# Branch C's head norm in three background pieces, with its factors and the output gate's rows sent round by DRAM

## The chip, the core and the metric

One core of a Trainium2 chip runs the whole program. The metric is device time in microseconds (us) from launch to end, as the median of several runs. The engines are named as the profile names them: PE (TensorE, with PEld for its weight loads), DVE (VectorE), ACT (ScalarE), POOL (GpSimd) and SP (SyncE, which issues every DMA of this kernel). All arithmetic is fp32. Matrix products split each operand into a high and a low part and take three products (`mm3`).

## What is computed

A two-layer mixer over 1152 tokens (128 context tokens, then 1024 latent ones) and 1024 channels. Each layer has three branches A (windowed attention), B (a gated recurrence) and C (differential attention). What the change touches is the norm at the end of branch C, and the gate of the residual:

```python
def diff_attn(q, k, v, lam, subln, lam_init):
    ...
        s = jnp.einsum('bqhmd,bshmd->bhmqs', qblk, k).astype(jnp.float32) * SCALE
        p = jax.nn.softmax(s, axis=-1)
        pd = p[:, :, 0] - lam * p[:, :, 1]
        return jnp.einsum('bhqs,bshe->bqhe', pd.astype(v.dtype), v)
    ...
    o = rmsnorm(o, subln) * (1 - lam_init)        # per token and head, over 128 channels

def mixer_tail(x, gate, oa, g_a, ob, g_b, oc, g_c, merge, P):
    m = jax.nn.sigmoid(merge).reshape(B, T, N_BRANCH, D_MODEL)
    y = (m[:, :, 0] * ((oa * jax.nn.silu(g_a)) @ P['w_br_a'])
         + m[:, :, 1] * ((ob * jax.nn.silu(g_b)) @ P['w_br_b'])
         + m[:, :, 2] * ((oc * jax.nn.silu(g_c)) @ P['w_br_c']))
    return x + gate * (y @ P['w_out'])            # gate: one row of 1024, from the modulation
```

## The kernel before

Tokens are nine tiles of 128, channels and heads lie on the 128 partitions where a product needs them. A layer has four stages.

1. **The unit phase** (`unit_phase`). Four heads of C, then branch A's four groups. A foreground does the attention of head h over five groups of token tiles (`GR`): scores and their eviction (`c_probs`), then, one group late, transposes and the product with V (`c_pv`, run by `flush`). A background generator makes the next head's q, k and v (`qkv_gemm`: nine token tiles, every third followed by `qk_rows`), then the head's SiLU gate in three pieces (`gate_silu`). `step(n)` takes n pieces of the background between groups; `fg` runs the foreground under a priority raised by 2000 instructions.
2. **The tail steps** (`tail_step`): 22 steps of merge gates and branch projections, with branch B's recurrence (`lru`) beside them.
3. **`tail_last`**: the last two column blocks, which use both `T` buffers (`mg2`).
4. **`w_out_phase`**: four column quarters `q4`, each over nine token tiles i: 24 products of 256 columns into PSUM, then on DVE `tm = p * gr` and `x = x + tm`, then a store. In layer 0 the next layer's modulation (`mod_chunk`, long sums on DVE) and its normed input (`to_h`) are made in the same stage.

The instruction order is not the program's: a planner simulates the program and takes, on each engine, the ready instruction of highest priority (program order, less the raised offset); that order is then fixed, and each engine runs its own list in order. SBUF buffers come from rings (`RINGS`: S 26, P 7, T 2, W 7, D 3, E 2, cx 1), PSUM from three (`PSB`: s 4, t 3, o 1). A tile waits until a slot of its ring is free.

At the end of head h of C, `c_finish` (L580) runs in the foreground, when the group after its last product is flushed, in head h+1's second group. It squares O (L582, ACT, one piece of 1152), sums over partitions with nine products against a column of ones (L585), takes the inverse root on DVE (`rsqrt`, 14 small instructions), spreads the nine factors over partitions with nine products of a broadcast column against the identity (L593), scales O from that PSUM (DVE) and multiplies by the gate on POOL. In the trace each fp32 product of these two lines stands as two matmuls, so 18 and 18 for a head. O sits in the P ring, the gate in the S ring, until then.

`gate_rows` (L1035) makes the row tile `gr` (128 x 2 x 256) of a quarter in the same way: four products of a broadcast column against the identity (L1040), two ACT copies. `gr` lies in the single `cx` buffer, so a quarter's copies wait for the last tile of the quarter before. The `xt` tiles of `w_out_phase` rotate over the rings E, D, T (`XT`), and in layer 0's last quarter over E, T (`XT3`).

Of the kernel before, what the change touches and what calls it, by code (L numbers as in the profile page):

```python
# [10 lines left out]
F32 = mybir.dt.float32  # L11
# [7 lines left out]
DEPTH = 2  # L19
# [45 lines left out]
def hybrid_dit_kernel(ctx, tc, I, O):  # L65
# [14 lines left out]
    def al(tag, name, *shape):  # L80

        return big.tile([128] + list(shape), F32, tag=tag, name=name, bufs=RINGS[tag])
# [33 lines left out]


    xres = drp.tile([NT, 128, DM], F32, name="xres")
    osp = [drp.tile([4, 128, NTOK], F32, name=f"osp{b}") for b in range(3)]
    xsp, gsp = (drp.tile([4, 128, NTOK], F32, name=n) for n in ("xsp", "gsp"))  # L120

# [456 lines left out]
        acopy(u.o[:, tiles[0] * 128:tiles[0] * 128 + w], po)  # L578

    def c_finish(L, u, h):  # L580
        sq = al("T", "sq", 1152)
        A.activation(out=sq, in_=u.o, func=AF.Square)  # L582
        p = ps("t", 9)
        for i in range(9):
            T.matmul(out=p[:, i:i + 1], lhsT=sq[:, i * 128:(i + 1) * 128], rhs=one, start=True, stop=True)  # L585
        e2 = tl("e2", 9)
        stt(e2, u.l0, EPS, u.l0, ALU.mult, ALU.mult)
        y = rsqrt(p, 9, 1.0 / 128, e2)
        for c in range(3):
            pb = ps("t", 3, 128)  # L590
            for t in range(3):
                i = 3 * c + t
                T.matmul(out=pb[:, t, :], lhsT=y[:, i:i + 1].to_broadcast([128, 128]), rhs=ident, start=True, stop=True)  # L593
            oc = u.o[:, c * 384:(c + 1) * 384].rearrange("p (t n) -> p t n", t=3)
            stt(oc, oc, L.D.sub1, pb, ALU.mult, ALU.mult)
            tt(Pq, u.o[:, c * 384:(c + 1) * 384], u.o[:, c * 384:(c + 1) * 384],
               u.gate[:, c * 384:(c + 1) * 384], ALU.mult)
        dma(osp[2][h], u.o)

# [126 lines left out]
    def unit_phase(L):  # L728

        l = L.l  # L730
        a_groups = [CQA, CKA, CVA]
        pend = None

        done = None

        def flush():
            nonlocal pend, done
            d, done = done, None
            if pend:
                pend()  # L740
                pend = None
            if d:
                d()

        def start(h):
            u = Unit()
            if h < 4:
                L.units.append(u)
                return qkv_gemm(L, u, L.wu, (0, 1), O["nck"][0, l, :, h, :, :], O["ncv"][0, l, :, h, :],
                                V if h == 0 else None)  # L750
            L.ua = u
            return qkv_gemm(L, u, L.wu, (2, 3), O["nak"][0, l], O["nav"][0, l].rearrange("t v d -> t (v d)"))

        def background():

            for h in range(4):
                L.wu = load_wu(L, c_groups(h + 1) if h < 3 else a_groups)
                yield from start(h + 1)
                yield from gate_silu(L, CGC + 128 * h, lambda gate, u=L.units[h]: setattr(u, "gate", gate))
            L.wu2 = load_wu(L, [CQA + 128, CQA + 256, CQA + 384])  # L760
            yield from a_gemm2(L)
            for g in range(4):
                yield from gate_silu(L, CGA + 128 * g, L.gates.append)
                if g:
                    yield from lru_x(L, g - 1)
            yield from lru_x(L, 3)

        def step(n):
            for _ in range(n):
                next(bg, None)  # L770

        def fg(f, *args):
            with tc.high_priority(offset=HPO):
                return f(*args)
        for _ in start(0):
            pass
        bg = background()
        step(BG0[0])
        fg(c_kconv, L, L.units[0], 0)
        for h in range(4):  # L780
            u = L.units[h]
            u.l0 = tl("l0", 9, bufs=2)
            qn = BGQ if h else BG0
            if h:
                step(qn[0])
            fg(v_conv, u, I["cache_c_v"][0, l, :, h, :])
            for g, tiles in enumerate(GR):
                n = len(tiles)
                q = fg(q_conv, u.q[:, tiles[0]:tiles[0] + n, :, :].rearrange("p t m d -> p (t m) d"), 2 * n)
                Ps = [fg(c_probs, L, u, tiles[0], q, 0)]  # L790
                fg(flush)
                if n == 2:
                    Ps.append(fg(c_probs, L, u, tiles[1], q, 1))

                def pend(u=u, tiles=tiles, Ps=Ps, h=h, g=g):
                    if g == 0:
                        u.o = al("P", "O", 1152)
                    c_pv(L, u, tiles, Ps)
                    if g == 4:
                        nonlocal done  # L800
                        done = lambda: c_finish(L, u, h)
                step(qn[g + 1])
            if h < 3:
                fg(c_kconv, L, L.units[h + 1], h + 1)
            else:
                fg(a_kconv, L)
        u = L.ua
        fg(v_conv, u, I["cache_a_v"][0, l].rearrange("t v d -> t (v d)"), True)
        fg(flush)
        L.mask = al("P", "mask", 9, 128)  # L810
        dma(L.mask, I["mask"].rearrange("p (a b) -> p a b", a=9))
        step(BGA[0])
        for g in range(4):
            for n, tiles in enumerate(GR):
                i, m = tiles[0], len(tiles)
                q = fg(q_conv, (u.qs[g] if g else u.q)[:, i:i + m, :, :].rearrange("p t h d -> p (t h) d"), 2 * m)
                Ps = fg(a_probs, L, g, tiles, q)
                fg(flush)

                def pend(g=g, n=n, tiles=tiles, Ps=Ps):  # L820
                    if n == 0:
                        L.Oa = al("P", "Oa", 1152)
                    a_pv(L, g, tiles, Ps, L.Oa)
                    if n == 4:
                        nonlocal done
                        done = lambda o=L.Oa: a_finish(L, g, o)
                step(BGA[n + 1])
        fg(flush)
        fg(flush)
        for _ in bg:  # L830
            pass
# [200 lines left out]
                tail_branch(L, 2, j, c, ohl, wbs[j], ms[j - 6][:, c, :])  # L1032
                y_split(L, j, c)

    def gate_rows(D, q4, dst):  # L1035

        for s in range(2):
            p = ps("t", 2, 128)
            for k in range(2):
                T.matmul(out=p[:, k, :], lhsT=D.modt[:, 16 + 2 * q4 + k, s:s + 1].to_broadcast([128, 128]),  # L1040
                         rhs=ident, start=True, stop=True)
            acopy(dst[:, s, :], p.rearrange("p k n -> p (k n)"), scale=0.5)

    def x_in(l, i):
        if l:
# [14 lines left out]
    def w_out_phase(L, Ln):  # L1060
        l = L.l
        wtag = ("P", "S", "S", "P")
        wq = [load_wo(L, 0, wtag[0])]
        gr = None
        for q4 in range(4):
            cs = slice(q4 * 256, (q4 + 1) * 256)
            if q4 < 3:
                wq.append(load_wo(L, q4 + 1, wtag[q4 + 1]))
            w = wq[q4]
            gr = al("cx", "gr", 2, 256)  # L1070
            gate_rows(L.D, q4, gr)
            if q4 == 1 and Ln is not None:
                load_unit_consts(Ln)
                Ln.wu = load_wu(Ln, c_groups(0))
# [112 lines left out]
    for l in range(DEPTH):  # L1187
        L = Ls[l]
        L.mods = [(L.D, 16, 3), (L.D, 19, 3), (L.D, 22, 2)] if l == 0 else []
        layer_scalars(L.D)  # L1190
        if l + 1 < DEPTH:
            for _ in layer_vectors(l + 1):
                pass
            Dn = Ls[l + 1].D
            L.mods += [(Dn, b, 3) for b in range(0, 24, 3)]
        unit_phase(L)
        steps = [(2, 0, j) for j in range(8)] + [(0, 1, j) for j in range(8)] + [(1, 2, j) for j in range(6)]
        o = {}
        for n, (br, order, j) in enumerate(steps):
            if n == 0:  # L1200
                with tc.high_priority(offset=TPO):
                    o[2] = load_o(L, 2)
            if n in LRUN:
                with tc.high_priority(offset=LPO):
                    lru(L, LRUN.index(n))
            if n == 7:
                with tc.high_priority(offset=TPO):
                    o[0] = load_o(L, 0)
            if n == 9:
                with tc.high_priority(offset=TPO):  # L1210
                    o[1] = load_o(L, 1)
            if n == STO:
                state_out(L)
            if n in MODN:
                with tc.high_priority(offset=MPO):
                    if L.mods:
                        mod_chunk(*L.mods.pop(0), "D")
            with tc.high_priority(offset=TPO):
                tail_step(L, br, order, j, o, 2 if n in LAG2 else MLAG)
        while L.late:  # L1220
            L.late.pop(0)()
        tail_last(L, 1, o[1])
        w_out_phase(L, Ls[l + 1] if l + 1 < DEPTH else None)

# [47 lines left out]
```

## Time and profile before

| | us |
|---|---|
| median of 3 runs (lowest, highest) | 2887.27 (2885.09, 2889.72) |
| the profiled execution | 2884.63 |
| its span, first to last instruction | 2882.8 |
| PE busy, DVE busy in that span | 2740.5, 1773.3 |

The profiled execution lies 2.64 us below the median, and 1.83 us of it lie outside the span. A busy PE is counted from matmul starts to modelled ends, which overlap, so the price of a matmul is read here from the distance between starts, not from its duration.

### The profile page before, as it was taken

How to read it: one execution, taken by the hardware profiler on the slowest of the kernel's cores; microseconds unless marked ns; L12 is line 12 of the kernel's file. 1: busy time of each engine (PE TensorE's matmuls, PEld its weight loads, DVE VectorE, ACT ScalarE, POOL GpSimd, SP SyncE). 2: the span in 40 equal slices, each digit the busy share in tenths (PEclk: the TensorE clock that was granted, in tenths of full speed). 3: DMA queues.
4: the chain of work that ended last, by engine and by line, in shares of the span. 5: the costliest groups of instructions: out<-in, count | busy, mean ns of one | idle time of the engine just before them, and what ended most of it. 6: DMA issues, size and time to landing. Idle time of an engine off the chain costs nothing.

```text
span 2882.8 us, 44242 instructions
## 1 busy us (share of the span) xinstructions
PE 2740.5 (95%) x16745; PEld 2648.5 (92%) x16745; DVE 1773.3 (62%) x4412; ACT 1284.2 (45%) x2577; POOL 924.8 (32%) x756
## 2 busy tenths in 40 slices
PE   8999999999998989998999999999999989999999
PEld 4889999999997989998989899998999989899989
DVE  5887878776646583116958887787665455311162
ACT  4464555566654631212144555555666456212110
POOL 1334354531234341213104252445212344322130
PEclk9999999999999999998999999999999999999999
DMA  6011011112222252114631010110112121311122
GB/s 228 25 33 34 19 32 42 36 48 74 70 73 65 65 159 68 52 39 144 195 100 36 22 34 19 33 48 31 55 64 80 63 70 60 114 44 49 49 90 85
DMA packets 231698, 190.74 MB, mean 66 GB/s; under 512 B 21746, under 2 KB 217660, under 8 KB 231484
## 3 DMA queue, kind: packets, MB, share of 16 engines
q1 hardware_dynamic: 231484, 187.92, 20.7%
q8 instruction: 131, 2.15, 0.3%
q14 instruction: 83, 0.68, 0.1%
HBM read 153.52 MB, written 34.35 MB: 65 GB/s over the span
## 4 chain that ended last, share of the span: by engine, by line
PE 71%; DVE 15%; ACT 5%; issue 4%; DMA 3%; POOL 1%; SPq 1%; DVEq 0%; ACTq 0%; POOLq 0%
PE ps_s L163 18%; PE ps_s L164 18%; PE ps_s L165 18%; PE ps_o L711 2%; PE ps_t L702 2%; DVE P L542 2%; PE ps_s L540 2%; DVE macc L112 2%; PE ps_t L569 1%; PE ps_s L541 1%; DMA modw<-in_mod_w_dram 1%; DVE lr L860 1%; DVE lr L112 1%; PE ps_o L164 1%; PE ps_s L662 1%
## 5 line engine op out<-in xcount | busy, mean ns | idle before, releaser
L163 PE MATMUL ps_s<-h,wsh 128*128 128x384 f32 x1920 | 660.0, 344 | 8.6 <-ACT mg L971 5.9
L165 PE MATMUL ps_s<-h,wsl 128*128 128x384 f32 x1920 | 654.4, 341 | 0.9 <-POOL wsl L103 0.9
L164 PE MATMUL ps_s<-h,wsh 128*128 128x384 f32 x1920 | 654.9, 341 | 0.0
L163 PEld LDWEIGHTS ps_s<-h,wsh 128*128 128x128 f32 x1920 | 364.3, 190 | 13.5 <-ACT mg L971 7.1
L165 PEld LDWEIGHTS ps_s<-h,wsl 128*128 128x128 f32 x1920 | 363.1, 189 | 2.0 <-POOL wsl L103 1.6
L164 PEld LDWEIGHTS ps_s<-h,wsh 128*128 128x128 f32 x1920 | 364.1, 190 | 0.6
L103 POOL TENSOR_TENSOR wsl<-wsraw,wsh 128x1024 fp32r<-128x1024 f32 x80 | 198.7, 2483 | 395.3 <-ACT wsh L100 229.6
L163 PE MATMUL ps_s<-uwh,h 128*128 128x384 f32 x864 | 296.9, 346 | 5.8 <-ACT h L100 2.8
L164 PE MATMUL ps_s<-uwl,h 128*128 128x384 f32 x864 | 293.9, 341 | 0.1
L165 PE MATMUL ps_s<-uwh,h 128*128 128x384 f32 x864 | 292.1, 344 | 0.0
L112 DVE SCALAR_TENSOR_TENSOR ps_s<-mg,ps_s 128x384 f32<-128x384 f32 x96 | 52.6, 559 | 359.7 <-PE ps_s L165 359.6
L103 POOL TENSOR_TENSOR qkraw<-qkraw,tab 128x384 f32<-128x384 f32 (+2 forms) x92 | 132.7, 1453 | 335.2 <-DVE qkraw L103 212.5
L542 DVE TENSOR_SCALAR_CACHE_REDUCE P<-ps_s 128x384 f32<-128x384 f32 (+1 forms) x400 | 205.5, 539 | 39.9 <-PE ps_s L541 38.7
L163 PE MATMUL ps_s<-oh,wb 128*128 128x384 f32 x576 | 196.0, 351 | 35.3 <-DVE yr L112 10.5
L103 DVE TENSOR_TENSOR PT<-ps_t,PT 128x512 fp32r<-128x512 f32 (+2 forms) x304 | 187.7, 625 | 59.5 <-ACT PT L100 58.0
L100 ACT ACTIVATE PT<-ps_t 128x512 fp32r<-128x512 f32 (+2 forms) x304 | 160.0, 546 | 125.1 <-PE ps_o L165 67.9
L552 ACT ACTIVATE P<-P,csm 128x1152 f32<-128x1152 f32 (+1 forms) x144 | 165.8, 1154 | 101.8 <-DVE csm L107 101.8
L164 PE MATMUL ps_s<-ol,wb 128*128 128x384 f32 x576 | 194.7, 346 | 0.0
L165 PE MATMUL ps_s<-oh,wb 128*128 128x384 f32 x576 | 194.5, 346 | 0.0
L971 ACT ACTIVATE mg<-ps_s 128x384 f32<-128x384 f32 x144 | 69.6, 485 | 266.1 <-PE ps_s L165 169.6
L163 PE MATMUL ps_s<-woh,yh 128*128 128x256 f32 x576 | 167.4, 291 | 11.7 <-DVE xt L103 6.5
L163 PEld LDWEIGHTS ps_s<-uwh,h 128*128 128x128 f32 x864 | 164.6, 191 | 9.4 <-ACT h L100 3.5
(253 smaller groups left out, 6364.6 us busy)
## 6 DMA issues: line engine op xcount, KB each, us to landing
wsraw<-in_w_in_dram SPq DMA_DIRECT2D x80, 512.0 KB, 3.7
wuraw<-in_w_in_dram SPq DMA_DIRECT2D x72, 192.0 KB, 3.5
ol<-osp SPq DMA_DIRECT2D x24, 576.0 KB, 5.0
modw<-in_mod_w_dram SPq DMA_DIRECT2D x16, 512.0 KB, 5.8
woraw<-in_w_out_dram SPq DMA_DIRECT2D x16, 512.0 KB, 4.4
modw<-in_mod_w_dram SPq DMA_DIRECT2D x14, 576.0 KB, 5.5
modw<-in_mod_w_dram SPq DMA_DIRECT2D x19, 384.0 KB, 4.3
wuraw<-in_w_in_dram SPq DMA_DIRECT2D x36, 128.0 KB, 2.3
```

The source lines that it names most:

```text
L100: A.activation(out=out, in_=in_, func=AF.Copy, scale=scale)
L103: e.tensor_tensor(out=out, in0=a, in1=b, op=op)
L112: V.scalar_tensor_tensor(out=out, in0=a, scalar=s, in1=b, op0=op0, op1=op1)
L163: T.matmul(out=out, lhsT=r(lh), rhs=r(rh), start=first, stop=False)
L164: T.matmul(out=out, lhsT=r(lh), rhs=r(rl), start=False, stop=False)
L165: T.matmul(out=out, lhsT=r(ll), rhs=r(rh), start=False, stop=last)
L540: T.matmul(out=p, lhsT=qh, rhs=kk, start=True, stop=False)
L542: V.tensor_scalar(out=S[:, n * c:n * c + n], in0=p, scalar1=1.0, scalar2=NEG, op0=ALU.mult, op1=ALU.max, accum_out=mx[:, mp, c:c + 1])
L552: A.activation(out=Ss[mp][:, 0:n], in_=Ss[mp][:, 0:n], func=AF.Exp, scale=0.125, bias=nm[:, mp:mp + 1], accum_out=acc)
L702: T.transpose(p[:, b, 128 * j:128 * j + 128], Ps[2 * t + j][:, (b0 + b) * 128:(b0 + b + 1) * 128], ident)
L711: T.matmul(out=po[:, t, :, :], lhsT=r(vs[kb]), rhs=r(x[:, b, :]), start=kb + k == 0, stop=k == 1 and kb == len(vs) - 1)
L971: A.activation(out=m, in_=p, func=AF.Tanh, scale=0.5)
```

## The change

`c_finish` becomes a generator that `flush` starts, and each `step` takes one piece of it after one piece of the background, so it runs at normal priority. Its Square and sums go in three pieces of 384 columns in D buffers, each sum copied from PSUM to `csum`. After `rsqrt`, one transpose turns the nine columns of factors into nine rows, ACT copies them, a DMA stores them to `ybd` in DRAM, and three DMAs load them back, each spread over all 128 partitions (192 KB) into a D buffer `yb`. DVE scales O from `yb`, POOL multiplies by the gate.

`gate_rows` becomes two transposes, one copy and one store to `gbd` for a whole layer, placed before `tail_last`; each quarter's `gr` is then loaded by two DMAs a quarter ahead, in `cx` for quarters 0 and 2 and in T for quarters 1 and 3.

```diff
+    ybd = drp.tile([4 * DEPTH, NT, 128], F32, name="ybd")
+    gbd = drp.tile([DEPTH, 8, 2, 128], F32, name="gbd")
...
     def c_finish(L, u, h):
-        sq = al("T", "sq", 1152)
-        A.activation(out=sq, in_=u.o, func=AF.Square)
-        p = ps("t", 9)
-        for i in range(9):
-            T.matmul(out=p[:, i:i + 1], lhsT=sq[:, i * 128:(i + 1) * 128], rhs=one, start=True, stop=True)
+        sums = tl("csum", 9)
+        for c in range(3):
+            sq = al("D", "sq", 384)
+            A.activation(out=sq, in_=u.o[:, c * 384:(c + 1) * 384], func=AF.Square)
+            p = ps("t", 3)
+            for t in range(3):
+                T.matmul(out=p[:, t:t + 1], lhsT=sq[:, t * 128:(t + 1) * 128], rhs=one, start=True, stop=True)
+            V.tensor_copy(sums[:, 3 * c:3 * c + 3], p)
+            yield
         e2 = tl("e2", 9)
         stt(e2, u.l0, EPS, u.l0, ALU.mult, ALU.mult)
-        y = rsqrt(p, 9, 1.0 / 128, e2)
+        y = rsqrt(sums, 9, 1.0 / 128, e2)
+        yield
+        p = ps("t", 128)
+        T.transpose(p[0:9, :], y, ident)
+        row = al("D", "yrow", 128)
+        acopy(row[0:9, :], p[0:9, :])
+        yd = ybd[4 * L.l + h]
+        dma(yd, row[0:9, :])
         for c in range(3):
-            pb = ps("t", 3, 128)
-            for t in range(3):
-                i = 3 * c + t
-                T.matmul(out=pb[:, t, :], lhsT=y[:, i:i + 1].to_broadcast([128, 128]), rhs=ident, start=True, stop=True)
-            oc = u.o[:, c * 384:(c + 1) * 384].rearrange("p (t n) -> p t n", t=3)
-            stt(oc, oc, L.D.sub1, pb, ALU.mult, ALU.mult)
...
+            oc = u.o[:, c * 384:(c + 1) * 384]
+            yb = al("D", "yb", 3, 128)
+            dma(yb, yd[None, 3 * c:3 * c + 3, :].to_broadcast([128, 3, 128]))
+            stt(oc, oc, L.D.sub1, yb.rearrange("p t n -> p (t n)"), ALU.mult, ALU.mult)
+            tt(Pq, oc, oc, u.gate[:, c * 384:(c + 1) * 384], ALU.mult)
         dma(osp[2][h], u.o)
+        yield
...
             if d:
-                d()
+                for _ in fin:
+                    pass
+                fin = d() or iter(())
...
             for _ in range(n):
                 next(bg, None)
+                next(fin, None)
...
-    def gate_rows(D, q4, dst):
+    def gate_rows(D):
+        p = ps("t", 2, 128)
         for s in range(2):
-            p = ps("t", 2, 128)
-            for k in range(2):
-                T.matmul(out=p[:, k, :], lhsT=D.modt[:, 16 + 2 * q4 + k, s:s + 1].to_broadcast([128, 128]),
-                         rhs=ident, start=True, stop=True)
-            acopy(dst[:, s, :], p.rearrange("p k n -> p (k n)"), scale=0.5)
+            T.transpose(p[0:8, s, :], D.modt[:, 16:24, s], ident)
+        row = al("D", "grow", 2, 128)
+        acopy(row[0:8], p[0:8], scale=0.5)
+        dma(gbd[D.l], row[0:8])
+
+    def gate_load(L, q4):
+        gr = al(("cx", "T")[q4 % 2], "gr", 2, 256)
+        for s in range(2):
+            dma(gr[:, s, :].rearrange("p (k n) -> p k n", k=2),
+                gbd[L.l, 2 * q4:2 * q4 + 2, s, :][None].to_broadcast([128, 2, 128]))
+        return gr
...
-            gr = al("cx", "gr", 2, 256)
-            gate_rows(L.D, q4, gr)
+            gr = grs[q4]
+            if q4 < 3:
+                grs.append(gate_load(L, q4 + 1))
...
+        gate_rows(L.D)
+        L.gr0 = gate_load(L, 0)
         tail_last(L, 1, o[1])
```

## Rows read from the trace of the kernel before

**Rows 1.** The page's part 1: busy us (share of span) xinstructions.
```profile
PE 2740.5 (95%) x16745; PEld 2648.5 (92%) x16745; DVE 1773.3 (62%) x4412; ACT 1284.2 (45%) x2577; POOL 924.8 (32%) x756
```

**Rows 2.** Busy time by stretch: six head periods with their sum; layer 0's output stage.
```profile
222.00:323.00 101.00, 97.76 (x623) 94.23 (x622) 78.14 (x243) 53.19 (x107) 42.23 (x43) 0.98 0.10 30
...
sum 609.00, PE 591.92 PEld 574.16 DVE 487.12 ACT 323.48 POOL 262.62; mean PE 98.65 PEld 95.69 DVE 81.19 ACT 53.91 POOL 43.77
...
1340.00:1515.00 175.00, 156.40 (x1160) 153.09 (x1161) 142.56 (x340) 51.70 (x152) 25.00 (x10) 0.92 0.48 149
```

**Rows 3.** PE's groups by line: xcount | busy us, mean ns | idle before us.
```profile
L593 PE MATMUL ps_t<-ident,rsq 128*128 128x128 f32 x144 | 17.6, 276 | 2.9 <-DVE rsq L112 2.9
L585 PE MATMUL ps_t<-one,sq 128*128 128x1 f32 x144 | 17.6, 245 | 1.0 <-ACT sq L582 0.8
L1040 PE MATMUL ps_t<-ident,modt 128*128 128x128 f32 x64 | 8.9, 277 | 0.0
```

**Rows 4.** Timeline of PE, layer 0's first finish: start us, us, instruction [idle before].
```profile
227.76 0.44 PE L540 MATMUL ps_s<-ck,qhl 128*128 128x384 f32 x1 [0.27 <-DVE P L542]
229.29 0.44 PE L540 MATMUL ps_s<-ck,qhl 128*128 128x384 f32 x1 [0.91 <-DVE P L542]
231.21 0.52 PE L164 MATMUL ps_s<-uwl,h 128*128 128x384 f32 x1
231.53 0.52 PE L165 MATMUL ps_s<-uwh,h 128*128 128x384 f32 x1
238.78 2.17 PE L593 MATMUL ps_t<-ident,rsq 128*128 128x128 f32 x18
240.71 0.42 PE L164 MATMUL ps_s<-uwl,h 128*128 128x384 f32 x1
```

**Rows 5.** First and last of five stretches of low clock: PEclk is the sixth figure.
```profile
230.70:234.10 3.40, 3.38 (x12) 3.38 (x12) 3.40 (x16) 1.50 (x4) 0.00 (x0) 0.50 0.00 0
...
1865.70:1869.10 3.40, 3.40 (x13) 3.40 (x12) 3.40 (x18) 0.00 (x0) 3.32 (x6) 0.50 0.07 22
```

**Rows 6.** Who PE waited for: us in total, times, longest.
```profile
PE ps_s L163 <- DVE xt L103: 6.5, 2, 3.6
PE ps_t L593 <- DVE rsq L112: 2.9, 2, 1.5
```

**Rows 7.** The chain that ended last, layer 1's output stage: start us, us, what.
```profile
2852.51 0.89 PE ps_t L1040 x8
```

**Rows 8.** Timelines of ACT and DVE, layer 0, first tile of quarter 1.
```profile
1397.72 0.83 ACT L100 ACTIVATE gr<-ps_t 128x256 f32<-128x256 f32 x2 [4.91 <-PE ps_t L1040]
1402.05 0.74 DVE L103 TENSOR_TENSOR xt<-ps_s,gr 128x256 f32<-128x256 f32 x2
```

**Rows 9.** DMA issues: xcount, KB each, median us to landing; then one engine's waits for loads.
```profile
osp<-O SPq DMA_DIRECT2D x8, 576.0 KB, 2.8
lg<-gsp SPq DMA_DIRECT2D x24, 192.0 KB, 4.2
xt<-in_x_sample_dram SPq DMA_DIRECT2D x32, 128.0 KB, 2.8
...
ACT uwh L100 <- DMA wuraw<-in_w_in_dram: 18.4, 10, 2.4
```

**Rows 10.** By tile: duration ns min/median/max of scaling from PSUM, scaling from SBUF, small steps.
```profile
L112 DVE SCALAR_TENSOR_TENSOR O<-O,sub,ps_t x24: 612/614/616, 239.7 to 1972.1; 128x384 f32<-128x384 f32 x24
L112 DVE SCALAR_TENSOR_TENSOR lr<-lr,lg x24: 526/834/2994, 866.7 to 2466.3; 128x384 f32<-128x384 f32 x24
L112 DVE SCALAR_TENSOR_TENSOR rsq<-ps_t,e x8: 165/167/170, 226.0 to 1967.3; 128x9 f32<-128x9 f32 x8
```

**Rows 11.** Timelines of DVE, ACT and SP in layer 0's last quarter.
```profile
1469.84 0.41 DVE L103 TENSOR_TENSOR xt<-ps_s,gr 128x256 f32<-128x256 f32 x1
1487.38 1.32 ACT L1111 ACTIVATE xlast<-xt 128x256 f32<-128x256 f32 x4
1487.82 0.81 SPq L97 DMA_DIRECT2D xt<-in_x_sample_dram  x2
```

More of the change, by code (lines that the diff above doesn't have):

```diff
@@ L580, in c_finish @@
     def c_finish(L, u, h):
-        sq = al("T", "sq", 1152)
-        A.activation(out=sq, in_=u.o, func=AF.Square)
-        p = ps("t", 9)
-        for i in range(9):
-            T.matmul(out=p[:, i:i + 1], lhsT=sq[:, i * 128:(i + 1) * 128], rhs=one, start=True, stop=True)
+        sums = tl("csum", 9)
[7 more added lines that the diff above has]
+            yield
         e2 = tl("e2", 9)
         stt(e2, u.l0, EPS, u.l0, ALU.mult, ALU.mult)
-        y = rsqrt(p, 9, 1.0 / 128, e2)
-        for c in range(3):
-            pb = ps("t", 3, 128)
-            for t in range(3):
-                i = 3 * c + t
-                T.matmul(out=pb[:, t, :], lhsT=y[:, i:i + 1].to_broadcast([128, 128]), rhs=ident, start=True, stop=True)
-            oc = u.o[:, c * 384:(c + 1) * 384].rearrange("p (t n) -> p t n", t=3)
-            stt(oc, oc, L.D.sub1, pb, ALU.mult, ALU.mult)
-            tt(Pq, u.o[:, c * 384:(c + 1) * 384], u.o[:, c * 384:(c + 1) * 384],
-               u.gate[:, c * 384:(c + 1) * 384], ALU.mult)
+        y = rsqrt(sums, 9, 1.0 / 128, e2)
[6 more added lines that the diff above has]
+        dma(yd, row[0:9, :])
+        for c in range(3):
+            oc = u.o[:, c * 384:(c + 1) * 384]
[3 more added lines that the diff above has]
+            tt(Pq, oc, oc, u.gate[:, c * 384:(c + 1) * 384], ALU.mult)
         dma(osp[2][h], u.o)
+        yield
     KROW = ((0, 1, 8, 2, 3, 8, 4, 5, 6), (5, 6, 7, 8))
@@ L734, in unit_phase @@
         done = None
+        fin = iter(())
         def flush():
-            nonlocal pend, done
+            nonlocal pend, done, fin
             d, done = done, None
@@ L1063, in w_out_phase @@
         wq = [load_wo(L, 0, wtag[0])]
-        gr = None
+        grs = [L.gr0]
         for q4 in range(4):
```

## The prediction

> **What bounds the kernel now.** I read the page's busy times first: PE is busy 95% of the span, DVE 62% [rows 1]. An average hides the stages, so the second view is the busy time by stretch. Over the six periods of a head of branch C that the trace shows whole, PE is busy 591.9 of 609 us, and DVE 487.1, which is 80% [rows 2]. There PE is the bound, but DVE has only about 20 us of slack in 101, and each engine works its list in order: a DVE instruction that waits holds up the score evictions behind it, and PE then runs out of PSUM. In layer 0's output stage the bound is mixed: PE 156.4 and DVE 142.6 of 175 us [rows 2]. Third come the groups of the lines that go, and the timeline for what one matmul costs.
>
> **PE instructions removed.** The 18 spreading matmuls of a head start at 238.78, and the next product starts at 240.71 [rows 4]: 1.93 us, 0.107 each. (The group's mean duration of 276 ns overlaps itself [rows 3].) They go, two matmuls of the one transpose come: 16 x 0.107 = 1.71 us a head, 8 heads, 13.7 us. The 144 one-column matmuls of L585 [rows 3] stay, in smaller lots. The gate rows' 64 matmuls [rows 3] become 2 x 2 a layer, 8 in all: 56 x 0.107 = 6.0 us; the chain that ended last has eight of them at 0.89 us [rows 7], 0.111 each, so they are on the path. Together -19.7 us. The 16 ACT copies of `gr` become 2, on an engine with idle time: nothing.
>
> **Waits that go.** In two heads PE waited for the inverse root before it could spread, 2.9 us [rows 6]; a background piece leaves no foreground product behind it: -2.9. The root ran at high priority on DVE in front of score evictions; in the first head that cost PE 0.27 + 0.91 us [rows 4]. With layer 1's like head, -2.4 (0 if the same small steps only hit later evictions). In layer 0, quarter 1's `gr` copy waited 4.91 us for its matmuls and the evictions came at 1402.05 [rows 8]; PE's second wait for them, 6.5 - 3.6 = 2.9 us [rows 6], belongs to this place. A row loaded a quarter ahead is not late. Bounds 0 (DVE is loaded with modulation sums there, and may evict no earlier) and -2.9; I take -2.
>
> **The clock.** After five of the eight finishes PE's granted clock is 0.50 (1.2 GHz) for 3.4 us [rows 5], before which PE ran one-column matmuls and short waits; products then start 0.32 us apart [rows 4]. At half speed 1.7 us are lost each time, 8.5 us in all. Smaller lots among full products may keep the clock up, but three finishes with the same 18 one-column matmuls show no such stretch, so these alone do not decide it. Bounds 0 and -8.5; I take half, -4.3.
>
> **What is added on DVE.** (a) 24 copies of three columns out of PSUM, about 0.17 each by the nine-column step [rows 10]: 4 us. (b) 24 scalings now read O and `yb` both from SBUF. From PSUM they took 612 to 616 ns without exception; the nearest row with two SBUF inputs of the same shape took 526 to 2994, median 834 [rows 10]. The median adds 24 x 0.22 = 5.3 us; the bounds are 24 x (526 - 614), -2.1 us, and 24 x 2.38, 57 us, if each met the longest. (c) Waits for `yb`. The trace has no scaling that waits on such a chain of two DMAs. From below: the 24 loads of `lg`, of the same 192 KB, land in 4.2 us [rows 9] and could all be asked for early, so 0. From above: ACT's waits for weight loads are 18.4 / 10 = 1.84 us each [rows 9], and 24 of them are 44 us. Here a load can be asked for only after the store of the factors has landed (2.8 us for `osp` [rows 9]), and only three D slots exist, of which `qk_rows` holds two; the planner will put the scaling where it expects the landing. I take a wait in half of the 24: 22 us. Queued behind each are score evictions, and PE waits for those.
>
> How much of DVE's time reaches PE? In the first finish the root's 14 small steps, at 0.17 us [rows 10] some 2.4 us, went in front of evictions, and PE lost 1.18 us [rows 4]: about half. Background work of lower priority fills idle DVE time, so I take 0.4 where a wait cannot be moved, and for (a) and (b) the same: 0.4 x (4 + 5.3 + 22) = +12.5 us.
>
> *A rule beside (b).* The Trainium skill (SBUF — State Buffer, Who interferes with whom) says that a VectorE instruction with two SBUF inputs contends with a GpSimd instruction that reads SBUF and one with a single SBUF input does not: the second of the two blocks until the first is done. The 2 ns to either side from PSUM and the spread from SBUF agree with it. By the rule a scaling would often sit out POOL's gate multiply of the third before it, and the term would be nearer its upper bound.
>
> **What is added elsewhere.** The Square in thirds costs ACT a little and stands in no one's way. 2 x 9 + 8 x 4 = 50 DMA issues go to SP, which issues nearly all through the span; 196 KB loads are small beside the transfers there. In the unit phase a load that waits for a landing holds the weight loads queued behind it on SP; these are asked for well ahead, so 0 (if not, another 1.84 a head). O and its gate stay until the last piece: by the code O(h-1) overlaps O(h) for at least one more group, the P ring then needs two O, two pending and three current tiles, which is 7 of 7. It fits, without spare: 0, with PE's background products as cover.
>
> **The T ring in layer 0's last quarter.** This is the place that speaks against the change. Quarter 3's row now lies in one of two T buffers, and tiles 1, 3, 5, 7 use T for `xt`. Before, tile 5 was evicted at 1469.84, while tiles 3 and 5 each held a T buffer; four `xlast` copies ran only at 1487.38, and the last two tiles' loads were issued at 1487.82 [rows 11]. With one buffer tile 5 can start only after tile 3's copy, some 18 us later, and tile 7 after tile 5: load 2.8, two DVE steps of 0.4, store 2.8 [rows 9], about 6.4 us more for the last third of the next layer's input. PE has the first third's products to do meanwhile. Bounds 0 (the planner finds other work) and +12 (twice that chain). I take +6.
>
> **Sum.** -19.7 - 2.9 - 2.4 - 2 - 4.3 + 12.5 + 6 = -12.8 us. On the profiled execution's own 2884.6 that is 2871.8; it stands 2.6 us under the median, so on 2887.3 the forecast is 2874 (0.45% faster). A change of 0.2%, 5.8 us, is about what a measurement of this kernel tells from none.
>
> **The rivals.**
> 1. *Everything is hidden and the clock stays up.* For it: the scaling that reads `lg` never waited for its load, and the clock's lows follow the old finish. Then -19.7 - 2.9 - 2.4 - 2.9 - 8.5 = -36.4, 2851. Against it: the load is asked for late, behind a store. 0.13.
> 2. *The head period is not PE's to shorten.* The foreground's own chain (DVE eviction, exponentials on ACT, transposes) fills the period with DVE at 80%, and the next head's keys come out of background DVE and POOL work; the 13.7 us of the finish then turn into idle PE, and only the gate's share and the waits count: about -12.8 + 13.7, +1, 2888, no change. Against it: PE's background products fill nearly all its idle time today. 0.19.
> 3. *DVE stands still for the landings* (slower). All 24 scalings wait, at 1.84 us, and PE pays in full since DVE is nearly as loaded: 44 us in place of the 12.5 x 22/31 = 8.8 charged for them: -12.8 + 35 = +22, 2910. It beats the gain once PE loses over 0.9 us a load ((12.8 + 8.8) / 24). For it: 1.84 us is what a planned load cost ACT when it was late. Against: background scalings come after ready foreground work. 0.20.
> 4. *It does not do what it says*: pieces left over are drained by `flush` in the foreground. By the code there are five pieces and five steps of the next head's groups before the next finish, so this gets no chance of its own.
>
> **Chances.** The forecast's case, 2860 to 2881, has 0.48, rival 1 has 0.13, so faster 0.61; rival 2, same 0.19; rival 3, slower 0.20. The range 2851 to 2900 takes in rivals 1 and 2 and half of rival 3; the forecast's own range is 2860 to 2881.
>
> **What would show it.** Right: in the groups by line the spreading matmuls gone, the head periods some 2 us shorter (101 to 99), few low-clock stretches at the finishes, and PE's gaps after the scaling under 0.5 us. Wrong: DVE rows that wait for `yb` with over 1 us each and score products behind them; head periods unchanged with more idle PE; the first products of layer 1 more than 6 us later against the end of layer 0's output products; `xt` waiting for T in the other quarters.

## The result, and the profile after

The changed kernel takes 2924.45 us (median of 4 runs, 2920.28 to 2926.41), the kernel before 2888.49 beside it (4 runs). The ratio is 1.012, 95% interval 1.010 to 1.0141: 36 us slower, where 2874 and 13 us faster were forecast, with 2851 to 2900 as the range.

The profiled executions differ by 2923.1 - 2882.8 = 40.3 us. First the page's part 1 of the kernel after, against [rows 1]:

```profile
PE 2746.8 (94%) x16549; PEld 2630.4 (90%) x16549; DVE 1806.0 (62%) x4436; ACT 1288.0 (44%) x2587; POOL 923.8 (32%) x756
```

196 matmuls are gone (each transpose stands in the trace as one matmul, where the prediction counted two and so 184). The weight loads fell by 18.1 us, yet PE is busy 6.3 us longer: its remaining matmuls stand longer in the trace, where their ends are modelled. To see what that is, take the distance from each matmul's start to the next one's and split it at the shape's usual distance, its pitch (0.174 us for 384 columns, 0.118 for 256, 0.109 for 128). The part up to the pitch fell by 18.9 us in all; the part beyond it, which is gaps, waits for evictions and low clock, rose by 59.2. The sum is +40.3. So the work went away as forecast, and was paid for three times over.

Where: busy time by stretch, from the second head's period to the end of branch A, per layer (us; then PE, PEld, DVE, ACT, POOL; the sixth figure is PE's granted clock). Before:

```profile
193.80:806.90 613.10, 599.03 (x3801) 579.71 (x3800) 449.44 (x1339) 353.06 (x783) 220.17 (x210) 0.99 0.14 43
1629.10:2240.60 611.50, 597.45 (x3801) 578.48 (x3801) 450.60 (x1339) 353.10 (x783) 220.02 (x210) 0.99 0.14 43
```

After:

```profile
197.50:828.60 631.10, 602.55 (x3732) 572.11 (x3732) 468.48 (x1351) 357.30 (x794) 219.60 (x210) 0.99 0.15 46
1652.00:2284.40 632.40, 602.22 (x3733) 573.07 (x3733) 465.15 (x1351) 357.56 (x794) 219.84 (x210) 0.99 0.15 46
```

These two stretches, called the *attention stretches* below, are 18.0 and 20.9 us longer: 38.9 of the 40.3. PE has 69 and 68 matmuls fewer in each and idles 28.6 and 30.2 us in place of 14.1 and 14.1. Of the 38.9, the six head periods that the stretches hold took 25.9, and branch A, in which the fourth head is finished, 13.0.

One head shows what happens in the change. Busy time by stretch, second head of layer 0, after:

```profile
245.80:255.80 10.00, 10.00 (x68) 9.01 (x67) 9.86 (x35) 2.43 (x4) 7.22 (x10) 1.00 0.01 2
255.80:265.80 10.00, 10.00 (x59) 10.00 (x59) 5.79 (x24) 6.52 (x14) 1.33 (x3) 1.00 0.00 0
265.80:285.80 20.00, 16.56 (x100) 13.73 (x99) 16.48 (x47) 8.58 (x15) 9.54 (x5) 1.00 0.41 116
```

The same 40 us before:

```profile
242.00:262.00 20.00, 19.75 (x128) 18.68 (x128) 17.59 (x57) 11.00 (x22) 3.76 (x4) 1.00 0.09 34
262.00:282.00 20.00, 19.93 (x131) 19.50 (x130) 13.43 (x42) 10.41 (x18) 14.04 (x13) 1.00 0.22 64
```

Before, PE starts 128 + 131 matmuls, foreground and projections mixed. After, it starts 68 + 59 + 100. In the middle stretch PE is full, but with projections alone, while DVE has little to do; in the last the foreground is left by itself, and PE goes at the pace of DVE's evictions, 100 matmuls where 131 were. The clock is 1.00 in all of them. PE's timeline shows the seam (start us, us, instruction):

```profile
266.90 0.34 PE L167 MATMUL ps_s<-uwh,h 128*128 128x384 f32 x1
267.08 0.27 PE L598 MATMUL ps_t<-ident,rsq 128*9 128x128 f32 x1
267.19 0.27 PE L444 MATMUL ps_t<-ident,qdup 128*128 128x128 f32 x1
267.29 0.49 PE L571 MATMUL ps_t<-ident,P 128*128 128x128 f32 x3
268.97 0.66 PE L571 MATMUL ps_t<-ident,P 128*128 128x128 f32 x4 [0.75 <-ACT yrow L100]
```

The foreground's transposes (L444, L571) stand right behind the piece's transpose of the factors (L598), which stands behind 72 projection products in a row, started from 254.59 on. In each of the six heads there are such runs of 48 and of 72, and both end in a piece's products; the kernel before has none longer than 39. This is what PE does here, but it is not yet the cause: a version without these runs loses as much (section 4). The same picture a group earlier, at the second third's sums, now with a wait:

```profile
242.29 0.38 PE L590 MATMUL ps_t<-one,sq 128*128 128x1 f32 x2 [1.99 <-ACT sq L587]
242.53 0.31 PE L444 MATMUL ps_t<-ident,qdup 128*128 128x128 f32 x1
```

PE stands 1.99 us for a Square that stands in ACT's list behind the Square of the projections' `qk_rows` (240.98, 0.84 us). Over the kernel, who PE waited for (us in total, times, longest):

```profile
PE ps_s L542 <- DVE P L544: 18.3, 27, 2.0
PE ps_t L590 <- ACT sq L587: 14.4, 9, 2.0
PE ps_t L571 <- ACT yrow L100: 4.5, 6, 0.8
PE ps_s L165 <- DVE xt L103: 3.6, 1, 3.6
```

The last row answers [rows 6]: 6.5 became 3.6 as forecast, and the wait for the root before the spread (2.9) is gone. Score evictions (L544) were 7.7 us, 14 times, before. And DVE's waits for the loaded factors, feared most in the forecast:

```profile
DVE O L112 <- DMA yb<-ybd: 4.7, 6, 1.3
```

### The profile page after: what moved, and what is told of

It is laid out like the page before. It is cut to its first block, busy times and chain, and to the rows that moved or that the text cites. A ratio compares the mean times of both kernels' runs of the same rounds, so it can differ in the third digit from the quotient of the medians.

```text
span 2923.1 us, 43956 instructions
## 1 busy us (share of the span) xinstructions
PE 2746.8 (94%) x16549; PEld 2630.4 (90%) x16549; DVE 1806.0 (62%) x4436; ACT 1288.0 (44%) x2587; POOL 923.8 (32%) x756
## 4 chain that ended last, share of the span: by engine, by line
PE 36%; DVE 8%; DMA 3%; ACT 3%; issue 2%; POOL 1%; SPq 0%; DVEq 0%; ACTq 0%; POOLq 0%
PE ps_s L165 9%; PE ps_s L166 9%; PE ps_s L167 9%; PE ps_s L542 1%; DMA xres<-xt 1%; DVE macc L112 1%; DVE P L544 1%; PE ps_o L723 1%; PE ps_t L571 1%; PE ps_t L714 1%; PE ps_s L543 1%; DVE lr L875 1%; DVE PT L103 1%; DVE rsq L103 1%; DMA wuraw<-in_w_in_dram 0%
## 5 line engine op out<-in xcount | busy, mean ns | idle before, releaser
L165 PEld LDWEIGHTS ps_s<-h,wsh 128*128 128x128 f32 x1920 | 364.7, 190 | 16.3 <-ACT mg L986 7.0
L103 POOL TENSOR_TENSOR qkraw<-qkraw,tab 128x384 f32<-128x384 f32 (+2 forms) x92 | 126.8, 1389 | 323.3 <-DVE csum L591 110.1
L544 DVE TENSOR_SCALAR_CACHE_REDUCE P<-ps_s 128x384 f32<-128x384 f32 (+1 forms) x400 | 203.5, 538 | 18.7 <-PE ps_s L543 18.4
```

The lines of the kernel that those rows point to most:

```text
L103: e.tensor_tensor(out=out, in0=a, in1=b, op=op)
L165: T.matmul(out=out, lhsT=r(lh), rhs=r(rh), start=first, stop=False)
L544: V.tensor_scalar(out=S[:, n * c:n * c + n], in0=p, scalar1=1.0, scalar2=NEG, op0=ALU.mult, op1=ALU.max, accum_out=mx[:, mp, c:c + 1])
```

## The experiments

Each ran beside the kernel before on the same chip; the ratio is to it, with its 95% interval. "Attention stretches" gives the sum of the two in the profiled run, 1224.6 before, 1263.5 after the change.

**1. The two parts apart.** Gate rows alone keeps the old `c_finish` called at once; norm alone keeps the old `gate_rows`.

> Only the gate rows' part of the change; the norm of branch C's heads stands as in the kernel before. Theory (the place of the norm's pieces costs all of the loss and the gate rows gain): the profiled kernels' stretches from the first product of the closing projection to the next stage are 0.9 and 1.3 us shorter and the ends of the second branches 0.2 and 2.3 us, so about 5 us faster than before: 2883 (2878 to 2887). Rival (the gate rows' loads share the blame, by the ring of large buffers and by 15 waits of 1 us of DVE for the residual rows): 2895 or more.

> Only the norm's part of the change; the gate rows are made as before, by 32 products. Theory: the whole loss is here, 36 plus the 5 that the gate rows gain, so 2929 (2922 to 2936). Rival (the gate rows share the blame): 2910 or less.

Measured: gate rows alone 2886.16, ratio 0.9992 (0.9983 to 1.0002); norm alone 2933.03, 1.0154 (1.0137 to 1.017). The loss is the norm's. The 5 us of gain for the gate rows were too much: no difference that can be told. Gate rows alone, 1227.5 in the attention stretches, is the base of the experiments below.

**2. Place against way.**

```
 thirds, PE spread:   pieces as in the change, then  T.matmul(pb, y[:, i].to_broadcast, ident) x9  as before
 foreground, DRAM:    Square, sums, root, row, store and loads in one go at high priority
```

> The change with the norm's thirds in the background by the small buffers as it has them, but the factors spread by nine products each head as before, with no row in DRAM and no loads of it. Theory (the place of the sums decides: TensorE's list stands 2 us at the one-column products behind a Square that stands in ScalarE's list behind the projections' evictions, and the small ring of three is held by the pieces so that the next head's keys come late): the loss stays, 2915 to 2930. Rival (the DRAM way decides: the row, three loads behind weight loads, small buffers held until they land): the loss is gone, about 2883 as with the gate rows alone, at most 2890.

> The change with the norm's sums as before (one Square into a large buffer, nine one-column products, all at once with high priority), the factors spread by DRAM and the small buffers, also at once with high priority. Theory (place decides): no loss, and 8 heads x 8 products fewer at 0.107 us = 7 us less than with the gate rows alone: 2876 (2868 to 2886). Rival (the DRAM way decides): ScalarE's and the small ring's waits for the landings come back in the foreground, 2905 or more.

Measured: 2931.45, 1.0151 (1.0135 to 1.0166), and 2936.00, 1.0162 (1.0145 to 1.0179). The first goes the place theory's way, 1.5 us above its range; the second is a miss for it. Sums in pieces without DRAM cost the time, the way by DRAM in the foreground costs it too, and the two together, as in the change, cost no more than either. At once by DRAM, DVE stands in the foreground for the landings, for longer than after the change (4.7 us, 6 times):

```profile
DVE O L112 <- DMA yb<-ybd: 14.1, 10, 3.7
```

What the rest of this second loss is stays open.

**3. Priority, slots and rings.** The first two take the pieces with `fg(next, fin, None)`; the second also moves `sq`, `yrow`, `yb` to ring E, as does the fourth for the foreground norm. The third adds empty pieces to the gate rows alone:

```
+  p = ps("t", 1); T.matmul(out=p, lhsT=ident, rhs=one); V.tensor_copy(tl("dum", 1), p); yield   # x4
```

> The change with its norm's pieces emitted in the same places between the projections' steps, but with the foreground's priority; buffers as in the change. Theory (a piece of low priority takes a PSUM slot of the ring of three that the transposes of the queries and of the probabilities use too; it stands in TensorE's list behind 72 projection products, and so the foreground tiles that come three slots later stand there as well: after the change the query transposes of head 1's fourth group come at 267.2, right behind the piece's own at 267.1, and its first evictions at 274.7 in place of 263.5): with high priority the loss of 36 is gone, 2870 to 2895. Rival (O stays in its ring of seven, and the gate rows in theirs, five steps longer, which holds the next scores up): the pieces stand in the same steps, so the loss stays, 2910 or more.

> As the run before, with high priority, and the squares, the row and the loaded factors taken from the ring of two middle buffers, which only the foreground uses in this stage, in place of the small ring of three that the projections' key and query rows use. Theory: whatever the small ring still costs in the run before goes too, 2868 to 2885. Rival (O's longer stay): 2910 or more.

> The gate rows' part alone, the norm as in the kernel before, and in the places of the change's pieces four empty ones of low priority per head: a PSUM tile of the ring of three, one one-column product of constants, one copy of 128x1 by VectorE; 32 of each in all. Their own work is 32 x (0.11 + 0.16) = 9 us if none of it is hidden. Theory (the slot taken at low priority holds the foreground up): 2905 or more, with the fourth groups of heads 1 to 3 some 8 us late. Rival (the Squares, the long stay of O, or the DRAM way cost the time): 2886 to 2895.

> The foreground norm with its factors by DRAM (2936), with the row and the loaded factors in the ring of two middle buffers in place of the small ring of three. Theory (in the small ring a loaded factor's buffer waits for the projections' rows of low priority to let go of theirs, and those for it): the loss goes, 2875 to 2895. Rival (the landings themselves, some 2 us each way, cost the time wherever they land): 2915 or more.

Measured: 2910.22 (1.0068, 1.0047 to 1.009); 2968.77 (1.0271, 1.0249 to 1.0293); 2909.16 (1.0065, 1.0047 to 1.0084); 2942.46 (1.0174, 1.0151 to 1.0197). Priority gives back 14 of the 36, not all: a miss for its theory, at the edge of the rival's range. Four empty pieces a head cost 23, as their theory has it, about twice their own work (64 matmuls of 0.11 and 32 copies of 0.16 us, 12 in all): their attention stretches are 621.7 and 622.1, +16.3, and DVE stands in its list for their products (who DVE's copy `dum` waited for):

```profile
  PE ps_t L741: 25.7, 12
```

The fourth groups, which that theory has some 8 us late in every head, came 6 to 8 us late in layer 1's three heads and not late in layer 0's, so its time came out better than its mechanism.

Both runs with ring E miss their forecasts. Ring E was a bad choice, since the queries' copies use it: ACT's `qdup` waited 41.8 us for scalings in the fourth run. So these two say nothing for or against the small ring.

**4. What does not cost it.** One edit each: the piece ahead of the background's step; the gate products put off to the fifth step, on the gate rows alone; O freed early (`tt(Pq, gate_c, o_c, gate_c)` in each third, the factors then scale the gate row).

> The change with one edit: in each step the norm's piece is emitted ahead of the projections' step in place of behind it, at the same low priority. Theory A (a piece's PSUM slot of the ring of three, taken behind a step's projection products, holds the foreground up): the transpose of the factors no longer stands behind the 72 products, the fourth groups come some 5 us earlier per head, 2895 to 2912. Theory B (O and the gate rows stay five steps longer in their rings): the stay is hardly shorter, 2918 to 2928.

> The gate rows' part alone, the norm at once with the foreground's priority as before, but its last step, the three gate products by GpSimd and the store, put off to the fifth step as in the change; so O and the gate row stay in their rings as long as after the change, and no engine has more to do. Theory A (PSUM slots): no loss, 2882 to 2890. Theory B (the stay of O in its ring of seven): most of the loss, 2905 to 2925.

> The change with the gate product moved ahead: each third's piece multiplies O into the gate row's buffer by GpSimd, the factors scale that buffer, and the store reads it; O is free after the third Square, the gate row as late as before; the same number of instructions. Theory A: no gain, 2918 to 2928. Theory B: the loss goes for the most part, 2885 to 2905.

Measured: 2930.62 (1.016, 1.0132 to 1.0188); 2886.55 (0.9997, 0.9987 to 1.0008); 2920.43 (1.0121, 1.0103 to 1.0138). The stay of O and the gate rows in their rings costs nothing, and freeing O early gains at most 4 us (nothing by the ratios, 1.0121 against 1.012). The order within a step is not it either, which is a miss for theory A: with the piece ahead, no run of projection products in those heads is over 25, and the loss is all there. So the runs of 48 and 72 that the change shows are not what the loss needs.

**5. The sums as idle work.** The old norm stays, and pieces that nothing uses stand in the change's places.

```
+  sq = al("D", "sq", 384); A.activation(out=sq, in_=<constants>, func=AF.Square)
+  p = ps("t", 3); T.matmul(p[:, t], sq[:, t*128:...], one) x3; V.tensor_copy(sums[:, 3c:3c+3], p); yield   # x3
```

Squares alone drops the second line; private has a Square of 96 columns in a buffer of its own; high runs them in the foreground's priority; not read has both Squares, and the products read the private one.

> The gate rows' part alone, the norm as before, and beside it the change's three pieces of sums in their places, of constants in place of O (a Square of 384 columns into the small ring, three one-column products into a PSUM tile, a copy), with nothing that uses them. Their own work in a layer: 12 Squares of 0.4 us, 36 products of 0.11, 12 copies of 0.16. Theory A, with what the four empty pieces cost (23): 20 to 35 more than the gate rows alone, 2906 to 2921. Theory B: their own work alone, at most 2895.

> The idle thirds (2945) with only the Squares left: three Squares of 384 columns per head into the small ring of three, at the pieces' places and priority, with no PSUM tile, no product and no copy. Theory P (what TensorE does for the pieces costs the time: products that stand in its list for the Square and hold a PSUM slot that the foreground's transposes come to next): about the gate rows alone, 2884 to 2893. Theory D (the small ring, which the projections' key and query rows need twice per group): 2915 to 2945.

> The idle thirds with their Square narrowed to 96 columns, in a buffer of its own in place of the small ring; the PSUM tiles, the three products and the copy (of 96 partitions) stay. Theory P: the loss stays for the most part, 2925 to 2945. Theory D: what the four empty pieces cost, 2900 to 2912.

> The idle thirds with the foreground's priority, in the same places. Theory P (it is the foreground that waits behind the pieces, and what a piece of high priority waits for is only its Square): 10 to 25 less than the idle thirds, 2920 to 2935, as high priority took 14 from the change. If priority makes no difference, 2940 to 2950.

> The idle thirds once more, with both Squares: the one of 384 columns into the small ring, which nothing reads, and the one of 96 columns in a buffer of its own, which the products read. So ScalarE, TensorE, VectorE and PSUM have as much to do as in the idle thirds (2945) and more, but a small buffer is free as soon as its Square is written, and not only when the products are. Theory P+D (a small buffer is held, 4.6 us in the mean and 7 to 9 in the worst piece of each head, until TensorE's list comes to the products, and the projections' rows wait for it): what the private Squares cost and no more, 2900 to 2912. Rival (the parts just add up in a crowded stage, whatever the buffer): 2935 or more.

| idle pieces | us | ratio (95%) | attention stretches over the base |
|---|---|---|---|
| whole | 2945.03 | 1.0203 (1.0187 to 1.0218) | +50.8 |
| Squares alone | 2885.61 | 0.9992 (0.9982 to 1.0001) | -4.6 |
| private, narrow | 2904.58 | 1.0065 (1.0048 to 1.0083) | +11.5 |
| whole, high | 2939.50 | 1.0182 (1.0163 to 1.0201) | +42.8 |
| not read | 2921.52 | 1.0103 (1.0081 to 1.0124) | +31.4 |

Three idle pieces of sums a head cost 59 us, more than the whole change does and more than either theory allowed; their 144 matmuls take 16 of it at 0.11 each. ACT's Square and the small ring alone cost nothing. The same chain of Square, products and copy without the small ring costs some 18, about its own matmuls; with the ring, far more than the sum. (The private Square is also the shorter one, 0.28 us against 0.51.) The whole idle pieces, attention stretches:

```profile
194.70:833.70 639.00, 617.78 (x3873) 594.24 (x3872) 462.57 (x1351) 359.06 (x794) 216.27 (x210) 0.98 0.13 42
1664.50:2303.80 639.30, 619.26 (x3874) 596.51 (x3873) 464.31 (x1351) 358.85 (x795) 219.06 (x210) 0.97 0.13 42
```

Squares alone:

```profile
195.40:811.00 615.60, 600.97 (x3802) 581.10 (x3801) 448.20 (x1339) 357.82 (x794) 219.94 (x210) 0.99 0.14 43
1636.10:2243.40 607.30, 595.15 (x3801) 576.46 (x3800) 451.39 (x1339) 357.88 (x794) 218.95 (x210) 1.00 0.14 44
```

A piece is a chain over three engines: ACT squares, PE sums, DVE copies. In the whole idle pieces each engine's list stands for another (waits of PE, ACT, and DVE's copy `csum`):

```profile
PE ps_t L744 <- ACT sq L741: 9.5, 8, 1.4
```
```profile
ACT sq L741 <- PE ps_t L744: 17.9, 2, 9.0
```
```profile
  PE ps_t L744: 16.0, 8
```

These rows do not say which wait costs the time: in the private pieces, which cost little, ACT waited 21.1 us and DVE 10.6 in the same two places, and only PE's wait for the Square is much less (2.3).

Not read misses its forecast of 2900 to 2912: to free the small buffer at once takes back 19 of the 51, not 39. So the hold is one share, and 20 us of the interplay stay without a single name. Priority, in the pieces marked high, takes back 6 of the 59, which lies between its two forecasts.

**6. Sums first, spread later; and private Squares in the change.** The first keeps Square, sums and root in the foreground as before and makes four background pieces of the rest. The second is the change with nine Squares of 128 columns through one buffer, and `rsq` with two buffers in place of three.

> The norm's sums and root at once with the foreground's priority as in the kernel before, and only the spread in the background: one piece with the transpose, the row and its store, three with a load, a scaling and a gate product each. Theory P (a single PSUM slot per head and no Square or one-column product in the background): the loss goes, 2875 to 2895, and it may beat the kernel before, by the 16 products a head that it lacks (14). Theory D (four small buffers held over landings): 2910 to 2935.

> The change itself with its Squares taken out of the small ring: nine of 128 columns per head, one after the other through one buffer of their own (for its room the ring of small root steps has two buffers in place of three); sums, places, priority, the row and the loads by DRAM as in the change. Theory P+D: the part of the loss that comes of held small buffers goes, 2895 to 2912; what is left is the PSUM slots and the rows and loads in the small ring. Rival (the small ring is not what costs the change its time): 2918 or more, and the nine Squares in a row may add to it.

Measured: 2898.43 (1.0044, 1.0029 to 1.0059) and 2963.48 (1.0258, 1.0239 to 1.0277). With the sums back in the foreground 26 of the 36 are gone (30 of the 36 by the attention stretches against the base), 3 us short of its theory's range. The spread by DRAM in the background then costs no wait (DVE waits 1.2 us in all for `yb`), but it does not pay the 14 us of its missing products either: its attention stretches are 619.5 and 613.6, 5.6 over the base, and most of the rest lies in a stage that it doesn't touch (last section). The second run settles nothing, since the smaller root ring put in a new wait:

```profile
PE ps_t L599 <- DVE rsq L112: 53.0, 8, 8.2
```

No version beat both kernels by more than can be told; the gate rows alone (0.9992) are level. One that keeps the old norm for the fourth head and spreads by DRAM later for the other three was not tried. A rival stays untested as well: every edit makes the planner fix new lists, and no run holds the lists of the other work as they were, so a loss by a worse order of that work was not told apart from a loss by the pieces' own waits. Squares alone and the stay of O show only that not every new order costs time.

## Why the prediction was wrong

**What held.** The instructions removed: -18.9 by the pitches against -19.7. The quarter's wait for `gr`: -2.9 in its row. The 24 copies: 0.155 us each, 3.7 for 4. The scalings: 21 of 24 took 0.61 us, as from PSUM, and three took more, +4.1 us in all for +5.3. The T ring: from the start of layer 0's last output product to layer 1's first exponential 92.1 us in place of 87.8 (91.2 with the gate rows alone, 87.6 with the norm alone), so +4.2 for +6. Gate rows in all: -2 forecast (-6.0 - 2 + 6), -2 measured and not to be told from 0.

**What was sized wrong on DVE.** Waits for `yb` took 4.7 us where 22 were taken, so rival 3 (2910) came nearest of the rivals by a way that did not happen: luck, not insight. DVE's busy time rose by 32.7 us all the same, for the most part through steps of the inverse root that the sum does not have (last section).

**The step that failed** is the pair of sentences that priced the pieces' place at nothing: "a background piece leaves no foreground product behind it", and "The Square in thirds costs ACT a little and stands in no one's way". The first is refuted by PE's timeline, where the foreground's transposes stand behind the piece's products twice a head; the second by PE's waits for that Square, 1.99 us in the row shown and 14.4 in all. The place was put at a gain of 2.9 + 2.4 us. What the runs show in its stead: the attention stretches grew by 38.9 us although some 14 us of products had left them; the same pieces of sums, idle beside the old norm, cost 59; and taking the sums back to the foreground returns 26 of the 36. So it is the sums in background pieces that cost the time. I had counted a piece by its instructions, and by the engine that was thought to be free. The prediction saw that only three D slots exist and that `qk_rows` holds two, but priced them for `yb` alone and not for the Squares.

How the pieces cost it is shown only in part. In the change, each engine works a fixed list in order, and the chain over ACT, PE and DVE makes one list stand for another. The foreground falls some 9 us behind within a head (the fourth group's first exponentials at 285.10 in place of 275.50, with 0.9 of lateness just before; of 3.7 at the head's start, 5.3 have become at its end), and the projections that should have filled its eviction pace are already spent: that is the 100 matmuls for 131. But the idle pieces say that handovers alone are not the price. With a buffer of its own the same chain adds 11.5 us to the stretches, less than its 16 us of matmuls; with the small ring 50.8, of which 19 go when the buffer is freed at once. So in the idle pieces the excess comes with the small ring, in part by its hold and in part in a way that no run names. Whether it is so in the change itself is not shown, since the run with private Squares there was spoiled by another ring. High priority mends 14 of 36 in the change and 6 of 59 in the idle pieces, so priority alone is not the cause. That a longer stay of O hurts, and that the way by DRAM is needed for the loss, fell.

**The clock**, put at -4.3, did not gain. In the attention stretches PE's granted clock was 0.50 (1.2 GHz) for 17.1 us before and 30.7 after, 8.5 and 15.4 us lost. But gate rows alone, with the old norm, stood there for 27.3 us, so one execution of each tells no difference; the mean granted clock was 0.973 to 0.980 in the executions of the kernel before that ran beside the experiments, and 0.976 to 0.977 after. In the whole idle pieces it was 61.4 us, so 30.7 lost: some 17 of their 50.8 us are low clock. No run tells whether that is a cause of the rest or comes of PE's waits.

**Rival 2** (the head period is not PE's to shorten) had the right kind, PE idle where DVE's chain sets the pace, and saw no loss in it.

## What to carry to other kernels

Price background work by what it shares with the work around it, and not by its instructions alone. Here a short chain over three engines, put between the pieces of a stage where PE is 98% and DVE 73% busy, cost about its own matmuls with a buffer of its own (18 us against 16), and 59 when its Square lay in a ring of three that the projections use. Before splitting a burst, try the pieces as idle work beside the old code; here one such run showed a loss of the right kind, and larger than the change's own. And read the weight loads' busy time beside PE's: they fell while PE's busy time rose, and the count of matmuls says that the work had fallen.

## What the runs showed of the hardware

**Small steps of DVE sit out POOL's instructions.** The program's inverse roots (the head norm's and those of `qk_rows` and of the input norms) have 702 steps, which took 143 us before and 179 after, more than all of DVE's rise (1773.3 to 1806.0). The whole difference is in steps over 0.6 us: 13 before (25.4 us together), 44 after (65.2), and all 57 end within 0.15 us of the end of a POOL instruction that was running. Timelines of DVE and POOL, after:

```profile
278.37 2.00 DVE L103 TENSOR_TENSOR rsq<-rsq 128x12 f32<-128x12 f32 x1
```
```profile
277.68 2.66 POOL L103 TENSOR_TENSOR uwl<-wuraw,uwh 128x1152 fp32r<-128x1152 f32 x1 [1.82 <-ACT uwh L100]
```

A step that usually takes 0.17 us takes 2.00 and ends with a POOL product that began 0.7 us before it. The Trainium skill (SBUF — State Buffer, Who interferes with whom) says that a VectorE instruction with two SBUF inputs, or a `tensor_scalar` in a two-port mode, blocks in full until a GpSimd instruction that reads SBUF and was first is done. 34 of the 44 have two SBUF inputs and agree; ten are `tensor_scalar`, of which no run shows the mode. The prediction weighed this rule for the 24 scalings, of which only three were long (1.52, 1.94, 2.64 us). The long steps are for the most part not the head norm's: 10 of the 44 have its nine columns (9.5 us; 3 and 3.7 us before), while 32 have the 12 or 6 columns of `qk_rows`, whose code the change left alone (50.7 us; 7 and 14.9 before), and the step shown is one of these. Spreading later had 25 long steps and lost little, the whole idle pieces 24 and lost 59 us, so these steps do not follow the loss, and no run shows what they alone cost.

**The clock of an untouched stage.** Layer 0's output products are the same in the gate rows alone and in sums first, spread later, and take 134.2 and 140.1 us at granted clocks of 0.96 and 0.91:

```profile
1344.60:1478.80 134.20, 120.22 (x968) 118.74 (x969) 111.00 (x232) 26.86 (x88) 21.49 (x8) 0.96 0.56 169
```
```profile
1350.00:1490.10 140.10, 126.16 (x967) 125.19 (x968) 112.35 (x232) 27.36 (x88) 20.66 (x8) 0.91 0.53 162
```

With 0.95 after the change itself and 0.91 with the whole idle pieces (139.8 us), this adds up to 6 us to a kernel, in a stage whose code is one and the same. Each figure is from one profiled execution, so it is not shown whether the clock here goes with the kernel or with the execution; comparisons here therefore go by the attention stretches too.
